# Order of the first transfers, of the key and query latents, and of the decays in a two-block transformer kernel

## The chip, the cores and the metric

The kernel runs on one core of a Trainium2 chip. The metric is the time of one execution on the device, in microseconds, as the median of several runs. Time before: 1764.14 us, median of 3 runs (1761.76 to 1773.75). Lower is better.

## The reference, cut to what matters

A first block of two layers (latent attention beside a gated mLSTM, then a convolutional feed-forward) works on 256 tokens of width 1024. A second block of one layer (linear attention, an RWKV recurrence and neighbourhood attention over a context of 256 tokens, then a mixture of 32 experts) follows. All numbers are float32. What the change touches is this:

```
silu_c, silu_cc = silu(c), silu(c_ctx)                 # one row of 1024 each
mod = silu @ ada_w + ada_b                             # 6 parts of 1024: shift, scale, gate, twice
h   = rms_norm(x) * gain * (1 + scale) + shift
# a mixer of the first block (two layers)
proj = h @ w_in                                        # c_q 384, c_kv 256, k_rope 32, q_m, k_m, v_m, o_m, i_m, f_m, gates
q  = (rms_norm(c_q)  @ w_uq ).reshape(.., 8 heads, 64 + 32);  q_rope  = rope(q[.., 64:])
kv = (rms_norm(c_kv) @ w_ukv).reshape(.., 8 heads, 64 + 64);  k_rope  = rope(k_rope)
y_mla   = softmax(q k^T / sqrt(96), masked by chunks of 64) @ v
y_mlstm = chunkwise mLSTM(silu(conv(q_m, k_m)), v_m, i_m, log_sigmoid(f_m))
          # cumulated log decays per head, running maxima, exp(decay) * (q k^T) @ v
x = x + gate * ((sigmoid(g) * (y_mla @ w1) + sigmoid(g') * (y_mlstm @ w2)) @ w_out)
```

The second block's context, `ctx_2`, goes through `mod`, `h` and a projection of its own; since it depends on nothing of the first block, the kernel does that first of all.

## The kernel before, in words

**Float32 by three products.** TensorE multiplies each operand as a rounded part and a rest: every weight tile of 128 rows and 1024 columns is split into `hi` (a cast on ScalarE, line 449) and `lo` (a difference on VectorE, line 451), and so are the activations. A product of a 128 by 128 weight block with 256 tokens is three matmuls (lines 472 to 474). Weights come from one long array in tiles of 2048 columns (1024 KB), through three buffers named `raw`; `Stream.take` loads a tile when it is first asked for and splits a half of it when that is first asked for.

**Modulation in the background.** `mod` is computed on VectorE: each 1024 KB tile of the `ada` matrix is loaded and multiplied with the activated row in two products with accumulation (line 532), each with a small read-out. Apart from the first two parts, this runs as a generator, one tile at a step; `tick()` moves it on by 0.8 tiles (first mixer) or 0.95 (second), and calls of `tick()` are spread over the mixer's text: one behind the norm, six in the latent stage, one per head, two per pair of heads in the mLSTM, four in the merge, four in the output projection. The tiles go through the same three `raw` buffers as the weights.

**Order.** The text of the program is not the order of the engines. When the program is built, a planner runs through it with modelled times and gives each engine, whenever that is free, the earliest instruction of the text that the model has as ready; each engine then works strictly in the order found. Loads of tiles stay in the order of the text on SyncE's queue. A table load that `pin()` asks for keeps its place in the text among the instructions of ScalarE.

**Start.** `context` (line 1157) activates the row `c_c` (`silu_row`, line 513: a transfer that spreads the row over all partitions, 512 KB, a tanh, a product, a halving), then runs eight modulation tiles through four buffers of their own. `vecs` (341.5 KB) and `ctxT` (1024 KB) are issued from ScalarE's queue, everything else from SyncE's. The second row, `c_x`, is activated behind the fourth tile (`CX_AT`). Then the context is normed (lines 589 to 593) and the joint projection of four columns begins, `proj4` (line 504), which takes the weights row by row so that it can start with the first normed block.

**Mixer** (line 659). *Latent stage:* `proj4` gives the three query latents and a fourth column that holds the gate inputs and k's rotary part (`p0`, `p1`); each latent is squared and scaled on ScalarE (`latent`, lines 683 and 684); `normed` (line 686) sums the squares by a matmul with ones, takes the root with logarithm and exponential, multiplies, and splits the result. Then the two key latents are projected (`p2`), evicted and normed. Four projections give q, two give k, one gives v. k's rotary part is spread to eight heads in one copy (line 728). *Decays* (lines 775 to 822): 26 VectorE instructions on 8 rows, some on other engines; they end in `rows`, `mcol` and `guard`, which only the mLSTM's pairs use. *Heads* (from line 839): scores, maximum, exponential, a step of the convolution generator (48 matmuls of projection, then convolution on VectorE), transposes and values. *Pairs* (line 873): the mLSTM. *Merge* (line 942) and *output projection* (line 960).

**PSUM.** The eight banks are shared out by tags: `d` two, `a` three, `y` two, `f` one. A bank holds two blocks of 256 tokens. `proj` and `proj4` use `d`.

The functions that the change touches:

## Time and profile before

| what | value |
|---|---|
| median of 3 runs | 1764.14 us |
| profiled execution, its own time | 1763.36 us |
| its span, first to last instruction | 1761.5 us |
| mean granted TensorE clock | 0.948 of full |
| busy: TensorE, VectorE, ScalarE, GpSimd | 1573.7, 1128.5, 756.8, 79.5 us |
| moved by DMA | 460.78 MB, mean 262 GB/s |
| the expert stage, 1310 to 1761 us | 403 GB/s, 0.99 of the DMA engines busy |

PE is TensorE, PEld its weight loads, DVE VectorE, ACT ScalarE, POOL GpSimd, SP SyncE. A busy TensorE is not one at its peak, since pipelined matmuls overlap in the record: the count of matmuls in a stretch tells more than the busy time. The clock is given as a share of full speed, 2.4 GHz; 0.5 is 1.2 GHz, and a mean between them is a stretch that had both. L472 is line 472 of the kernel before. In the rows below `<-` inside a name reads "written from", and in brackets behind an instruction stand the idle time before it and what ended it.

### The profile page before, as it was taken

How to read it: one execution, taken by the hardware profiler on the slowest of the kernel's cores; microseconds unless marked ns; L12 is line 12 of the kernel's file. 1: busy time of each engine (PE TensorE's matmuls, PEld its weight loads, DVE VectorE, ACT ScalarE, POOL GpSimd, SP SyncE). 2: the span in 40 equal slices, each digit the busy share in tenths (PEclk: the TensorE clock that was granted, in tenths of full speed). 3: DMA queues.
4: the chain of work that ended last, by engine and by line, in shares of the span. 5: the costliest groups of instructions: out<-in, count | busy, mean ns of one | idle time of the engine just before them, and what ended most of it. 6: DMA issues, size and time to landing. Idle time of an engine off the chain costs nothing.

```text
span 1761.5 us, 32047 instructions
## 1 busy us (share of the span) xinstructions
PE 1573.7 (89%) x13278; PEld 1267.9 (72%) x13278; DVE 1128.5 (64%) x2172; ACT 756.8 (43%) x1254; POOL 79.5 (5%) x81
## 2 busy tenths in 40 slices
PE   2988999999998899999999999999989867776766
PEld 2988999899998799989999999877874312221211
DVE  7998867798887998689988788757652111111011
ACT  3666545664455655556454566455531100000000
POOL 0000000020110000001011101000000000000000
PEclk7999999999999999999999999999989889887888
DMA  9846754556564678565667543223469999999998
GB/s 391 321 177 247 263 216 168 199 194 228 214 254 166 231 257 301 195 212 192 237 227 281 198 158 129 73 99 134 164 236 419 419 416 416 417 416 419 418 416 343
DMA packets 76807, 460.78 MB, mean 262 GB/s; under 512 B 8562, under 2 KB 11122, under 8 KB 28146
## 3 DMA queue, kind: packets, MB, share of 16 engines
q1 hardware_dynamic: 74064, 451.05, 67.1%
q10 hardware_dynamic: 2594, 7.64, 1.2%
q8 instruction: 106, 1.74, 0.4%
q14 instruction: 43, 0.35, 0.1%
HBM read 457.61 MB, written 1.05 MB: 260 GB/s over the span
## 4 chain that ended last, share of the span: by engine, by line
PE 65%; DMA 22%; DVE 8%; ACT 3%; issue 2%; SPq 0%; POOL 0%; DVEq 0%; ACTq 0%; POOLq 0%
DMA ew<-in_wgu 12%; PE d L472 11%; PE d L474 10%; PE d L473 10%; DMA ew<-in_wdown 7%; PE y L472 3%; PE y L474 3%; PE y L473 3%; PE a L1386 3%; DVE lo L451 2%; DVE raw L532 2%; PE d L2046 2%; PE a L1975 1%; PE d L485 1%; PE d L487 1%
## 5 line engine op out<-in xcount | busy, mean ns | idle before, releaser
L449 ACT CAST hi<-raw 128x1024 fp32r<-128x1024 f32 x309 | 322.5, 1049 | 307.5 <-PE d L473 178.8
L451 DVE TENSOR_TENSOR lo<-raw,hi 128x1024 fp32r<-128x1024 f32 x309 | 379.1, 1234 | 90.4 <-ACT hi L449 88.3
L472 PE MATMUL d<-hhi,hi 128*128 128x256 f32 x1352 | 396.9, 295 | 23.1 <-ACT hhi L590 20.8
L474 PE MATMUL d<-hhi,lo 128*128 128x256 f32 x1352 | 390.4, 289 | 5.3 <-DVE lo L451 5.3
L473 PE MATMUL d<-hlo,hi 128*128 128x256 f32 x1352 | 389.9, 289 | 2.2 <-DVE hlo L593 2.2
L472 PEld LDWEIGHTS d<-hhi,hi 128*128 128x128 f32 x1352 | 264.7, 196 | 31.7 <-ACT hhi L590 22.9
L474 PEld LDWEIGHTS d<-hhi,lo 128*128 128x128 f32 x1352 | 264.9, 196 | 7.8 <-DVE lo L451 6.5
L473 PEld LDWEIGHTS d<-hlo,hi 128*128 128x128 f32 x1352 | 265.2, 196 | 5.1 <-DVE hlo L593 2.9
L2046 PE MATMUL d<-ew,xe 128*32 128x512 f32 x984 | 167.9, 715 | 54.6 <-DMA ew<-in_wgu 54.2
L532 DVE SCALAR_TENSOR_TENSOR raw<-raw,cb 128x1024 f32<-128x1024 f32 x160 | 193.7, 1230 | 4.3 <-DMA raw<-in_ada 3.7
L2046 PEld LDWEIGHTS d<-ew,xe 128*32 128x32 f32 x984 | 26.4, 116 | 170.2 <-DMA ew<-in_wgu 145.6
L2051 DVE SCALAR_TENSOR_TENSOR moa<-moa,d 128x512 f32<-128x512 f32 x8 | 5.5, 688 | 179.8 <-ACT moa L2050 179.8
L2064 PE MATMUL y<-ew,mht 128*32 128x512 f32 x472 | 69.6, 652 | 28.8 <-DMA ew<-in_wdown 24.4
L2082 DVE SCALAR_TENSOR_TENSOR x<-f,mod_l,x 128x256 f32<-128x256 f32 x32 | 14.0, 479 | 126.3 <-PE f L2078 126.3
L457 POOL TENSOR_TENSOR hidl<-fgel,hidh 128x256 fp32r<-128x256 f32 x44 | 56.0, 1272 | 830.1 <-ACT hidh L456 765.1
L472 PE MATMUL y<-hhi,hi 128*128 128x256 f32 x320 | 91.6, 286 | 0.8 <-ACT hi L449 0.8
L474 PE MATMUL y<-hhi,lo 128*128 128x256 f32 x320 | 90.9, 285 | 0.8 <-DVE lo L451 0.8
L473 PE MATMUL y<-hlo,hi 128*128 128x256 f32 x320 | 90.6, 283 | 0.0
L2050 ACT ACTIVATE moa<-d 128x512 f32<-128x512 f32 x8 | 4.8, 597 | 186.1 <-PE d L2046 186.1
L2064 PEld LDWEIGHTS y<-ew,mht 128*32 128x32 f32 x472 | 12.8, 115 | 76.5 <-DMA ew<-in_wdown 56.0
L472 PEld LDWEIGHTS y<-hhi,hi 128*128 128x128 f32 x320 | 61.3, 192 | 1.4 <-ACT hi L449 1.0
L474 PEld LDWEIGHTS y<-hhi,lo 128*128 128x128 f32 x320 | 61.2, 192 | 1.4 <-DVE lo L451 1.0
(676 smaller groups left out, 3187.4 us busy)
## 6 DMA issues: line engine op xcount, KB each, us to landing
raw<-in_ws SPq DMA_DIRECT2D x151, 1024.0 KB, 4.9
ew<-in_wgu SPq DMA_DIRECT2D x100, 1024.0 KB, 18.0
raw<-in_ada SPq DMA_DIRECT2D x80, 1024.0 KB, 4.9
ew<-in_wdown SPq DMA_DIRECT2D x46, 1024.0 KB, 19.7
ew<-in_wgu SPq DMA_DIRECT2D x46, 512.0 KB, 13.8
ew<-in_wdown SPq DMA_DIRECT2D x28, 512.0 KB, 12.6
two<-in_wgu SPq DMA_DIRECT2D x20, 256.0 KB, 8.4
two<-in_wdown SPq DMA_DIRECT2D x16, 256.0 KB, 7.9
```

The lines of the kernel that those rows point to most:

```text
L449: f.append(nc.scalar.copy(hi_, raw))
L451: f.append(nc.vector.tensor_tensor(lo_, raw, hi_.bitcast(F32), OP.subtract))
L457: (eng or self.nc.vector).tensor_tensor(lo, src, hi.bitcast(F32), OP.subtract)
L472: nc.tensor.matmul(out, whi, hhi, start=first and i == 0, stop=False, **s)
L473: nc.tensor.matmul(out, whi, hlo, start=False, stop=False, **s)
L474: nc.tensor.matmul(out, wlo, hhi, start=False, stop=last and i == n - 1, **s)
L485: nc.tensor.matmul(out, hhi[:, tok], whi, start=first and i == 0 and not (t and shared), stop=False, **s)
L487: nc.tensor.matmul(out, hlo[:, tok], whi, start=False, stop=last and i == n - 1, **s)
L532: nc.vector.scalar_tensor_tensor(w, w, 1.0, c, OP.mult, OP.mult, accum_out=mod[:, j : j + 1])
L1386: nc.tensor.matmul(ps[r, g * 64 : g * 64 + 64], l_(g, p, r), r_(g, p, r), start=True, stop=True, skip_group_check=True)
L2046: nc.tensor.matmul(ps[32 * e : 32 * e + 32, :], xe[:, k, 32 * e : 32 * e + 32], w[e], start=k == 0, stop=k == 7, skip_group_check=True)
L2064: nc.tensor.matmul(py[q][32 * e : 32 * e + 32, :], ht[:, f * P + 32 * e : f * P + 32 * e + 32], w[e], start=f == 0, stop=f == 3, skip_grou ...
```

## The change

At the start, `vecs` and `ctxT` are issued on SyncE's queue behind the second modulation tile; the first weight tile of the context projection is loaded and its first half split behind the sixth tile (`Stream.reach`); the row `c_x` is loaded and activated behind the eighth. The halving in `silu_row` is gone, and the products of `ada` halve instead.

In each mixer the columns of the latents are reordered: `proj4` gives the two key latents and two query latents; the third query latent and the gate column follow in a bank of tag `y`. Key latents are normed there and then; the first half of k is projected, then the query latents are normed, then come the second half of k, its rotary part, v, and last q. The weights of `uq` are packed in that order. The six calls of `tick()` of the latent stage are gone. The decays are a function that is called in the second head (`hd == 1`), between the convolution step and the values; only their first four instructions stay in the latent stage.

```
--- before.py
+++ after.py
@@ _lat_cols
-    return r(0) + r(7) + z(24) + r(8) + z(24) + kr + kr[16:] + kr[:16] + r(1)
+    return r(1) + r(0) + r(7) + z(24) + r(8) + z(24) + kr + kr[16:] + kr[:16]
@@ prep
-        w.add("uq" + s, _tblk(f["w_uq"][l], _uq_cols()), _tblk(ukv[:, :512]), _tblk(ukv[:, 512:], n=512))
+        w.add("uq" + s, _tblk(ukv[:, :512]), _tblk(ukv[:, 512:], n=512), _tblk(f["w_uq"][l], _uq_cols()))
@@ class Stream
     def take(self, w=P):
 
-        net, a = self.net, self.pos
+        o = self.reach(self.pos)
         self.pos += w
+        assert o + w <= 1024
+        return self.hi[:, o : o + w], self.lo[:, o : o + w]
+
+    def reach(self, a=0):
+        net = self.net
         c, o = a // 2048, a % 2048
...
             self.hi, self.lo = net.split_w(self.raw[:, 1024 * b : min(1024 * b + 1024, self.width)])
-        o %= 1024
-        assert o + w <= 1024
-        return self.hi[:, o : o + w], self.lo[:, o : o + w]
+        return o % 1024
@@ silu_row
         nc.vector.scalar_tensor_tensor(t, th, 1.0, t, OP.add, OP.mult)
-        nc.vector.tensor_scalar(t, t, 0.5, None, OP.mult)
@@ ada
-                    nc.vector.scalar_tensor_tensor(w, w, 1.0, c, OP.mult, OP.mult, accum_out=mod[:, j : j + 1])
+                    nc.vector.scalar_tensor_tensor(w, w, 0.5, c, OP.mult, OP.mult, accum_out=mod[:, j : j + 1])
@@ mixer
-        raw = mt([8, T], "raw", F32, "kf")
+        raw = mt([8, T], "raw", F32, "qf")
...
-        def normed(dst, j, n, d):
+        def normed(dst, j, n, d, pin=True):
...
-            self.rstd(r, o, d)
+            self.rstd(r, o, d, pin=pin)
...
-        p0, p1 = self.proj4(st, h)
-        latent(0, p0[:, :T], self.V("qn" + s, 0))
-        latent(1, p0[:, T:], self.V("qn" + s, 1))
-        latent(2, p1[:, :T], self.V("qn" + s, 2))
-        self.tick()
-
+        pkv, p01 = self.proj4(st, h)
+        for q in range(2):
+            latent(3 + q, pkv[:, q * T : q * T + T], self.V("kvn" + s, q))
+        for q in range(2):
+            latent(q, p01[:, q * T : q * T + T], self.V("qn" + s, q))
+        p2 = self.ps("y")
+        self.mm3(p2[:, :T], st, h)
+        normed(ckv, 3, 2, 256)
+        latent(2, p2[:, :T], self.V("qn" + s, 2))
+        self.mm3(p2[:, T:], st, h)
+
+        cqp, ckvp = self.parts(cq, range(3)), self.parts(ckv, range(2))
+        kf, vn = mt([8, T], "kf"), mt([2, 512], "vn")
+        st = Stream(self, "uq" + s)
+
+        def keys(b):
+            pq = v2(self.proj(st, ckvp))
+            nc.scalar.copy(kf[0:64, 4 * b : 4 * b + 4 : 2, :], pq[0:64])
+            nc.vector.tensor_copy(kf[0:64, 4 * b + 1 : 4 * b + 4 : 2, :], pq[64:128])
+
+        keys(0)
+        normed(cq, 0, 3, 384, False)
+
+        krm = mt([T], "krm")
+        nc.vector.tensor_tensor(krm[64:128, :], p2[64:128, T:], self.cs[64:128, :], OP.mult)
         gi, gf = self.tmp(T, "gi", bufs=1, rows=8), self.tmp(T, "gf", bufs=1, rows=8)
-        nc.vector.tensor_scalar(gi, p1[0:8, T:], self.V("gb" + s)[0:8], None, OP.add)
-        nc.vector.tensor_scalar(gf, p1[32:40, T:], self.V("gb" + s)[32:40], None, OP.add)
-        krm = mt([T], "krm")
-        nc.vector.tensor_tensor(krm[64:128, :], p1[64:128, T:], self.cs[64:128, :], OP.mult)
-        self.tick()
-        normed(cq, 0, 3, 384)
-        p2 = self.proj(st, h)
-        for j in range(2):
-            latent(3 + j, p2[:, j * T : j * T + T], self.V("kvn" + s, j))
-        self.tick()
-        normed(ckv, 3, 2, 256)
+        nc.vector.tensor_scalar(gi, p2[0:8, T:], self.V("gb" + s)[0:8], None, OP.add)
+        nc.vector.tensor_scalar(gf, p2[32:40, T:], self.V("gb" + s)[32:40], None, OP.add)
+        keys(1)
         pk = self.ps("a")
         nc.tensor.matmul(pk[:, :T], self.C("rep")[64:128, :], krm[64:128, :], start=True, stop=True)
+        nc.scalar.copy(kf[64:128], bcn(pk[64:128, :T], 8))
+        pv = [self.ps("d") for _ in range(2)]
+        self.mm3n(pv, st, ckvp, 512, False)
+        for i in range(2):
+            nc.scalar.copy(vn[:, i, :], pv[i])
+        qf = mt([8, T], "qf")
+
+        lf, e1 = gf, self.tmp(T, "e1", bufs=1, rows=8)
+        nc.vector.tensor_scalar(e1, gf, -1.0, None, OP.mult)
+        nc.vector.tensor_tensor(e1, e1, gf, OP.min)
+        nc.scalar.activation(e1, e1, AF.Exp)
+        nc.scalar.activation(e1, e1, AF.Ln, bias=self.one[:8])
         for b in range(4):
             pq = v2(self.proj(st, cqp))
             nc.scalar.copy(qf[0:64, 2 * b : 2 * b + 2, :], pq[0:64])
             nc.vector.tensor_tensor(qf[64:128, 2 * b : 2 * b + 2, :], pq[64:128], bcn(self.cs[64:128, :], 2), OP.mult)
-            if b == 1:
-                nc.scalar.copy(kf[64:128], bcn(pk[64:128, :T], 8))
-            if b % 2:
-                self.tick()
-        for b in range(2):
-            pq = v2(self.proj(st, ckvp))
...
-        pv = [self.ps("d") for _ in range(2)]
-        self.mm3n(pv, st, ckvp, 512, False)
...
-        self.tick()
...
-        lf, e1 = gf, self.tmp(T, "e1", bufs=1, rows=8)
...
-        nc.vector.tensor_scalar(lf, gf, 0.0, None, OP.min)
...
-        nc.scalar.activation(guard, mcol[:, 1], AF.Exp)
+        rows, mcol, guard = mt([384], "mrows", F32R), mt([2, 2, 8], "mcol"), mt([2, 8], "guard")
+
+        def decays():
+            nc.vector.tensor_scalar(lf, gf, 0.0, None, OP.min)
...
+            nc.scalar.activation(guard, mcol[:, 1], AF.Exp)
...
             next(conv, None)
+            if hd == 1:
+                decays()
             self.pv(py, e, vn, hd)
             self.tick()
@@ context
             cc = self.silu_row(A["c_c"], nc.sync)
-            nc.scalar.dma_start(self.vec, A["vecs"])
             xc = cx.tile([P, 8, T], F32, name="xc")
-            nc.scalar.dma_start(xc, A["ctxT"].rearrange("p (k t) -> p k t", k=8))
+            st = Stream(self, "cx")
             for i, _ in enumerate(self.ada(A["ada2"], cc, self.V("adab2", 0, 48), self.mod_c, (0, 1), cx)):
-                if i == CX_AT:
-                    self.cb = self.silu_row(A["c_x"], nc.sync)
-            if CX_AT > 7:
-                self.cb = self.silu_row(A["c_x"], nc.sync)
+                if i == 1:
+                    nc.sync.dma_start(self.vec, A["vecs"])
+                    nc.sync.dma_start(xc, A["ctxT"].rearrange("p (k t) -> p k t", k=8))
+                if i == 5:
+                    st.reach()
+            self.cb = self.silu_row(A["c_x"], nc.sync)
             h = self.norm_mod(xc, self.V("n1", 0, 8), self.mod_c[:, 8:16], self.mod_c[:, 0:8], False)
-            st = Stream(self, "cx")
```

## Rows read from the trace of the kernel before

**Rows 1.** Windows: start:end, length, then busy us (instructions) of PE, PEld, DVE, ACT, POOL; clock; DMA.
```profile
0.00:10.00 10.00, 0.00 (x0) 0.00 (x0) 2.77 (x14) 2.34 (x2) 0.19 (x4) 1.00 0.81 290
...
20.00:30.00 10.00, 0.00 (x0) 0.00 (x0) 8.85 (x16) 2.25 (x2) 0.00 (x0) 0.56 1.02 424
...
122.00:156.00 34.00, 27.21 (x166) 24.37 (x164) 29.12 (x50) 23.54 (x37) 0.00 (x0) 0.85 0.65 247
156.00:200.00 44.00, 41.37 (x326) 39.01 (x325) 41.55 (x88) 26.39 (x56) 0.00 (x0) 1.00 0.62 223
284.00:313.00 29.00, 28.40 (x238) 27.97 (x238) 24.71 (x37) 15.24 (x19) 0.00 (x0) 1.00 0.51 182
579.00:605.00 26.00, 22.24 (x159) 20.55 (x157) 25.31 (x43) 19.31 (x32) 0.00 (x0) 0.93 0.69 254
605.00:620.00 15.00, 11.18 (x59) 9.76 (x59) 12.25 (x28) 6.85 (x14) 0.00 (x0) 0.77 0.59 221
737.00:767.00 30.00, 29.40 (x246) 28.98 (x246) 25.41 (x44) 15.79 (x21) 0.00 (x0) 1.00 0.51 176
```

**Rows 2.** Chain of waits, first 41 us: start, us, engine, tile, line, pieces.
```profile
3.43 16.41 DMA cb<-in_c_x
...
22.29 1.23 DVE cb L519
...
25.27 8.03 DVE raw L532 x14
...
33.81 2.07 DVE two L589 x5
...
39.44 1.15 DVE lo L451
40.63 0.58 PE d L474
```

**Rows 3.** Timeline of TensorE, first mixer: start, us, instruction, idle before and releaser.
```profile
122.38 0.28 PE L473 MATMUL d<-hlo,hi 128*128 128x256 f32 x1
122.50 0.28 PE L474 MATMUL d<-hhi,lo 128*128 128x256 f32 x1
...
126.95 0.58 PE L472 MATMUL d<-hhi,hi 128*128 128x256 f32 x1 [0.57 <-ACT hi L449]
...
149.59 0.39 PE L472 MATMUL d<-lat,hi 128*128 128x256 f32 x1 [1.87 <-DVE qf L726]
```

**Rows 4.** Timeline of ScalarE, latent stage of the first mixer.
```profile
122.15 0.38 ACT L683 ACTIVATE sqk<-d 128x256 f32<-128x256 f32 x1 [6.98 <-PE d L474]
...
124.19 1.28 ACT L540 ACT_TABLE_LOAD   x1
...
129.12 0.83 ACT L456 CAST lat<-raw 128x768 fp32r<-128x768 f32 x1
...
145.16 1.87 ACT L728 COPY kf<-a 64x2048 f32<-64x2048 f32 x1
```

**Rows 5.** Timelines of ScalarE and TensorE in the expert stage, around 1365 us.
```profile
1365.01 0.37 ACT L1991 COPY selT<-a 128x256 f32<-128x256 f32 x1 [12.05 <-PE a L627]
...
1365.43 0.61 PE L1993 MATMUL a<-ones,selw 128*128 128x1 f32 x4 [0.46 <-ACT selT L1991]
```

**Rows 6.** Windows of line 532 alone (modulation products and read-outs): VectorE, clock, DMA.
```profile
122.00:156.00 34.00, 7.26 (x12) 0.85 0.65 247
...
284.00:313.00 29.00, 0.00 (x0) 1.00 0.51 182
579.00:605.00 26.00, 8.18 (x14) 0.93 0.69 254
```

**Rows 7.** Timelines of VectorE and TensorE, second mixer, decays and first head.
```profile
600.63 0.41 DVE L776 TENSOR_TENSOR gf<-gf,e 8x256 f32<-8x256 f32 x1
...
611.04 1.13 DVE L813 TENSOR_TENSOR mrows<-mrr,mrows 8x384 fp32r<-8x384 f32 x2
...
612.97 0.47 PE L627 MATMUL a<-kon,esm 128*128 128x128 f32 x1 [3.82 <-ACT esm L851]
```

More of the change, by code (lines that the diff above doesn't have):

```diff
@@ L31 @@
 OUT_RATES = (0.4, 1.0, 1.0, 0.5)
-CX_AT = 3
 HG, MID_FIRST, MID_BUFS, RK_SECOND = "fy", 3, 4, (3, 0)
@@ L722, in mixer @@
-        st = Stream(self, "uq" + s)
+        nc.scalar.copy(kf[64:128], bcn(pk[64:128, :T], 8))
[8 more added lines that the diff above has]
+        nc.scalar.activation(e1, e1, AF.Exp)
@@ L726, in mixer @@
             nc.vector.tensor_tensor(qf[64:128, 2 * b : 2 * b + 2, :], pq[64:128], bcn(self.cs[64:128, :], 2), OP.mult)
-            if b == 1:
-                nc.scalar.copy(kf[64:128], bcn(pk[64:128, :T], 8))
-            if b % 2:
-                self.tick()
-        for b in range(2):
-            pq = v2(self.proj(st, ckvp))
-            nc.scalar.copy(kf[0:64, 4 * b : 4 * b + 4 : 2, :], pq[0:64])
-            nc.vector.tensor_copy(kf[0:64, 4 * b + 1 : 4 * b + 4 : 2, :], pq[64:128])
-        pv = [self.ps("d") for _ in range(2)]
-        self.mm3n(pv, st, ckvp, 512, False)
-        for i in range(2):
-            nc.scalar.copy(vn[:, i, :], pv[i])
-        self.tick()
         qk, vm = mt([8, T], "qk"), mt([2, 8, 65], "vm")
@@ L767, in conv @@
                 yield
-        lf, e1 = gf, self.tmp(T, "e1", bufs=1, rows=8)
-        nc.vector.tensor_scalar(e1, gf, -1.0, None, OP.mult)
-        nc.vector.tensor_tensor(e1, e1, gf, OP.min)
-        nc.scalar.activation(e1, e1, AF.Exp)
-        nc.scalar.activation(e1, e1, AF.Ln, bias=self.one[:8])
-        nc.vector.tensor_scalar(lf, gf, 0.0, None, OP.min)
-        nc.vector.tensor_tensor(lf, lf, e1, OP.subtract)
-        b = self.tmp(T, "bcum", bufs=1, rows=8)
-        nc.vector.tensor_tensor_scan(b, self.C("reset")[:8], lf, 0.0, OP.mult, OP.add)
@@ L788, in mixer @@
-        nc.vector.tensor_copy(sml[:, 4:8], cml)
-        bl = self.tmp(4, "mbl", bufs=1, rows=8)
-        nc.vector.tensor_copy(bl, blast)
-        nc.vector.tensor_tensor_scan(sml[:, 1:4], sml[:, 4:7], bl[:, 0:3], 0.0, OP.max, OP.add)
-        nm = gi
-        nc.vector.tensor_tensor(ch(nm), ch(cm), sml[:, 0:4].unsqueeze(2).to_broadcast([8, 4, 64]), OP.max)
-        nc.vector.scalar_tensor_tensor(ng, nm, -1.0, b, OP.mult, OP.subtract)
-        nc.vector.tensor_scalar(nm, nm, -1.0, None, OP.mult)
@@ L796, in mixer @@
-        off = self.tmp(16, "moff", bufs=1, rows=8)
-        ov = off.rearrange("p (c d) -> p c d", c=4)
-        nc.vector.memset(off, NEG)
-        for c in range(4):
-            nc.vector.memset(ov[:, c, c : c + 1], 0.0)
-            if c:
-                nc.vector.tensor_scalar(ov[:, c, :c], ov[:, c - 1, :c], bl[:, c - 1 : c], None, OP.add)
-        rows, rr = mt([384], "mrows", F32R), self.tmp(384, "mrr", bufs=1, rows=40)
-        nc.gpsimd.memset(rows.bitcast(F32), 0.0)
-        c4 = lambda t: t.rearrange("p (c s) -> p c s", s=64)
@@ L807, in mixer @@
-        for g in range(2):
-            r = slice(32 * g, 32 * g + 8)
-            for i, at in enumerate((0, 4)):
-                nc.vector.tensor_tensor(c4(rr)[r, at : at + 4 - 2 * i], ch(nm)[:, 2 * i :],
-                                        ov[:, 2 * i :, 2 * i + g].unsqueeze(2).to_broadcast([8, 4 - 2 * i, 64]), OP.add)
-            nc.scalar.copy(rows[r, :], rr[r, :])
-            nc.vector.tensor_tensor(rows[64 + 32 * g : 72 + 32 * g, :], rr[r, :], rows[r, :].bitcast(F32), OP.subtract)
@@ L814, in mixer @@
-        nc.gpsimd.memset(vm[:, :, :, 64:], 1.0)
-        pm = self.ps("a")
-        for k in range(2):
-            for i in range(2):
-                self.transpose(pm[:, (2 * k + i) * 8 : (2 * k + i) * 8 + 8], mrow[:, k * T + i * P : k * T + i * P + P])
-        mcol = mt([2, 2, 8], "mcol")
-        nc.vector.tensor_copy(mcol, pm[:, :32].rearrange("p (k i h) -> p k i h", k=2, i=2))
-        guard = mt([2, 8], "guard")
-        nc.scalar.activation(guard, mcol[:, 1], AF.Exp)
+        rows, mcol, guard = mt([384], "mrows", F32R), mt([2, 2, 8], "mcol"), mt([2, 8], "guard")
```

54 lines of the change are left out of this document (43 added, 11 removed).

## The prediction

> **What bounds the kernel now.** I read the busy times by stage first, then the chain of waits for the first 41 us, then TensorE's own timeline where a stage holds fewer matmuls than its length would take. The reader is to compare counts, not busy time. At full clock one 256-column matmul follows the other at 0.12 us [rows 3]. The latent stage of the first mixer holds 166 matmuls in 34.00 us [rows 1]; at that pace they take 19.9 us, so 14.1 us are lost there. The same stage of the second mixer holds 159 in 26.00 us (19.1 us at that pace, 6.9 lost), and the 15.00 us behind it, with the first head, hold 59 at a mean clock of 0.77 (7.1 us at that pace, 7.9 lost) [rows 1]. The last figure flatters the loss by some 1.4 us, since 12 of these matmuls are 512 wide: 6.5. So about 27 us of the two mixers are TensorE waiting or running at 1.2 GHz. In the first mixer its stream stops at 122.50 and is taken up at 126.95, because latents are evicted, squared and normed before anything else can be multiplied; later it waits 1.87 us for a VectorE copy of q [rows 3]. In the second it waits 3.82 us for the softmax of the first head, with the last of the decays just ahead on VectorE [rows 7]. VectorE is the second bound: 41.55 busy of 44.00 us in the first heads, 24.71 of 29.00 and 25.41 of 30.00 in the two merge stages [rows 1].
>
> The start is a chain of its own: the transfer of c_x, its activation, modulation products back to back, the norm, a low part of the first weight tile, and only at 40.63 the sustained stream of matmuls [rows 2].
>
> **The change, part by part.**
>
> *Start.* Ahead of the last modulation products now stand c_c (0.52 MB), vecs (0.35), ctx (1.05), eight tiles of 1.05 and, new, the first weight tile of 1.05; c_x goes behind them. That is 11.4 MB. The core moved 2.9 MB in its first 10 us and 424 GB/s later, with SyncE's queue alone at work from 20 to 30 us [rows 1], so putting vecs and ctx on that queue costs no bandwidth. By these rates the eighth tile lands at about 30. A product with its read-out takes 1.15 us (7 of each are the 14 pieces of 8.03 us), so its two end 2.3 us later; bias and gain took 0.5 (33.30 to 33.81), and the norm's first product starts at about 32.8 against 33.81 [rows 2]: 1.0 us. VectorE no longer sets this time, so the halving pass that is dropped there (over the same 1024 columns as the product of 1.23 us [rows 2], so at most that, twice here and once in the feed-forward) is worth nothing by itself. The larger part is the weight tile: it is split during the modulation products, so the stream need not wait for the low part (1.15 us, up to 40.6 [rows 2]). TensorE can then run its stream once the first low part of the normed context exists, five products and one more step of 0.41 us behind the start (2.5 us), at 35.3, against 40.63 less the 0.8 us of four matmuls done before: 4.5 us. Against it stands c_x: a table load, its tanh and its product of 1.23 us [rows 2] now fall among the norm's first instructions, and on SyncE its transfer stands behind a tile that waits for a buffer. I take **-4 us**, with ends of -1 (only the norm's advance) and -7. vecs and ctx land later by some 2 us; the bias and a sum of squares need them, some 10 us later.
>
> *Latent stage.* Key latents come first, and 48 matmuls (5.8 us) of the third query column and the gate column follow into a bank that needs no eviction. ScalarE evicts four latents instead of three (three took 122.15 to 124.19, 2.04 us [rows 4], so 2.7), loads a table (1.28 [rows 4]), and only then the third query latent (0.7): 4.7 us behind the joint projection.
>
> The gate column is written into the other half of the PSUM bank from which ScalarE reads that query latent. What this does shows elsewhere in the trace: a one-column matmul into a bank began 0.05 us after ScalarE's copy out of other columns of it, having waited 0.46 us [rows 5]. So I let the gate column wait: 24 matmuls take 2.9 us, the eviction ends at 4.7, a stop of about 2 us.
>
> The Trainium skill has the rule (PSUM — Partial Sum Buffer, "PSUM bank collisions raise a hardware error"): guard PSUM by bank and quadrant, not by address, so disjoint columns of a bank are no protection. By that rule the stop stands; if it did not hold, the 48 matmuls would run through and the sum below would be -17 instead of -13. The trace agrees with it, by the 0.46 us above.
>
> The norm of key latents runs meanwhile. Before, the cast of the normed latents began 7.0 us behind the first eviction [rows 4]; with the cast and its difference, 0.8 each, that is 8.6, and the gate column ends at 4.7 + 2.9 = 7.6. So the keys may wait 1 us more. Then the values wait for both key evictions, which may stand behind the 1.87 us copy of k's rotary part [rows 4], 1.0; the queries wait for the values' eviction, 0.6 (an estimate: a quarter of that copy's columns, and some start), and for their own, 0.9. 5.5 us of loss remain. First mixer: 14.1 - 5.5, **-8.5 us**, ends -3 and -12. Second: 6.9 + 6.5 - 5.5, less 2 for a stop that the decays make at head two instead of head one, **-6 us**, ends -2 and -10.
>
> *Decays.* 26 VectorE instructions, from the one at 600.63 to the pair at 611.04 [rows 7], 6.8 us in all, now come in one block inside the second head, where VectorE has 2.45 us free in 44.00 [rows 1]. Behind them on VectorE wait the next head's maximum and the convolution; the cover is that head's 48 matmuls. Part of them (in the second mixer the pair at 611.04) ran among the heads before. First mixer **+1.5 us** (0 to 5); the second's is in the figure above.
>
> *Six ticks less per mixer.* Each tick moves the modulation stream on by 0.8 or 0.95 of a tile. It took 7.26 and 8.18 us of VectorE in the latent stages [rows 6], which become free. The stream is not shorter: it ends six ticks later, and about three tiles (6 products, 7 us) reach into the merge stage, which had none [rows 6] and where VectorE has 4.3 and 4.6 us free [rows 1]. Overflow 3 us, part of it taken up by the output projection behind: **+2 us** per mixer, +4 (0 to 8); if that cover were gone, the whole 7 would be on the path. The same holds for transfers: three raw buffers serve weights and modulation tiles alike, so the latent stage's weights lose a rival and the merge's gain one; nothing.
>
> Sum: -4 - 8.5 - 6 + 1.5 + 4 = **-13 us** on the profiled execution's 1763.36 (its span of 1761.5 and 1.9 around it), which is 0.8 us under the median of the runs. All of it lies ahead of the expert stage, whose transfers start from where the work before them ends, so it passes to the end. I say 1750.
>
> **The rivals.**
>
> A, *the moved work fits*: merge and heads take it into VectorE's idle time (for it: the lagging stream leaves the heads less modulation work too), so +5.5 falls away and the start gains up to 7: 1742 to 1745. Without the wait within the bank it would be 4 less, 1738. Chance 0.20.
>
> B, *handed back, or not done as written*: the order on an engine is laid out by a planner's modelled times. It may put the queries' norm ahead of the keys', or ScalarE's evictions and casts pace the stage. Then the latent stages give 3 and 2, the start 3, and the costs stay: -8 + 5.5, about 1761. Against it: the gate column needs nothing but one eviction. Chance 0.20.
>
> C, *VectorE becomes the bound in heads and merge*, slower: the decays' 6.8 and the stream's 7 lie on the path whole in both mixers (28 us), and each pause sends the clock to 1.2 GHz as the first head of the second mixer had it (0.77 over 15 us, some 3.4 us [rows 1]), twice. With B's gains of 8: 28 + 7 - 8 = +27, about 1790. It decides once the block needs more than the free time of the first heads. For it: 2.45 us free of 44.00 [rows 1]. Against: part of the decays ran there before. Chance 0.07, most of it beyond 1%.
>
> **How the numbers follow.** The forecast has 0.53, and a range of its own of 1741 to 1760. A change within 1%, 17.6 us, can't be told from none by a measurement of this kernel; the limits are 1746.5 and 1781.8. Faster: nearly all of A and a third of the forecast, 0.38. Slower: 0.05. Same: 0.57. The range of 1734 to 1765 takes in A, the forecast and most of B.
>
> **What would show it.** In the changed kernel's trace: the sustained matmuls start near 35 to 36 us, with the first weight's low part ahead of the norm's products; after each mixer's joint projection 24 matmuls, a stop of about 2 us that an eviction ends, 24 more, then keys; no 3.82 us stop before the first softmax, but a shorter one behind the second head; no modulation products in the latent stages and about six in each merge; the clock at 2.4 GHz through both latent stages. It is wrong if the stop before the keys is as long as the old one (4.45 us), or if TensorE's waits for VectorE in the merge exceed 4 us.

## The result, and where the time went

The changed kernel takes 1773.01 us (median of 12 runs, 1764.24 to 1778.01) against 1761.89 (12 runs) for the kernel before: a ratio of 1.0052, 95% interval 1.0031 to 1.0074 (ratios here weigh all runs of both kernels; the medians alone would give 1.0063). It is slower by half a per cent, 23 us above the forecast of 1750 and 8 above the top of the range of 1734 to 1765. Its profiled execution took 1772.79 us with a span of 1770.9, 9.4 more than before. One run of 3644.1 us, of the kernel with the decays ahead of the heads, is left out of that kernel's ratio.

To find 9.4 us, cut both traces at the same events and subtract. The marks here are the context's last matmul, the first matmul of each mixer, its first head, its first pair, its merge, the last update of x, the next norm, the first expert matmul and the end. All lengths are in us.

| stretch | before | after | difference | forecast |
|---|---|---|---|---|
| start, to the context's last matmul | 108.4 | 110.2 | +1.8 | -4, with the next row |
| from there to the first mixer's first matmul | 0.8 | 5.7 | +4.9 | |
| first mixer, to the first head | 46.8 | 37.2 | -9.6 | -8.5 |
| its heads; its pairs | 69.0; 59.0 | 70.0; 58.7 | +1.0; -0.3 | +1.5; 0 |
| its merge and output projection | 48.4 | 51.4 | +3.0 | +2 |
| feed-forward | 231.6 | 231.2 | -0.4 | 0 |
| second mixer: norm to first head; heads | 40.8; 75.4 | 38.6; 69.8 | -2.2; -5.6 | -6 in all |
| its pairs | 57.5 | 57.6 | +0.1 | 0 |
| its merge and output projection | 48.8 | 59.5 | +10.7 | +2 |
| feed-forward | 235.0 | 235.5 | +0.5 | 0 |
| second block, up to the experts | 296.4 | 301.3 | +4.9 | 0 |
| experts | 443.8 | 444.2 | +0.4 | 0 |

The latent stages won what was forecast, or a little more. Three places lost more than forecast: the start (+6.7 instead of -4), the second mixer's merge and projection (+10.7 instead of +2) and the second block, whose text is untouched (+4.9 instead of 0).

The windows of the changed kernel (columns as in [rows 1]) show two of the three:

```profile
116.00:153.00 37.00, 33.28 (x240) 31.12 (x241) 28.52 (x50) 25.88 (x43) 0.00 (x0) 0.96 0.33 117
153.00:223.00 70.00, 67.32 (x545) 64.20 (x545) 63.01 (x128) 40.26 (x84) 0.00 (x0) 1.00 0.67 245
282.00:309.00 27.00, 24.79 (x204) 24.01 (x203) 26.86 (x43) 13.38 (x17) 0.00 (x0) 1.00 0.68 245
730.00:759.00 29.00, 26.79 (x207) 25.95 (x207) 25.60 (x41) 13.21 (x18) 0.00 (x0) 0.94 0.68 249
759.00:790.00 31.00, 27.55 (x198) 26.45 (x196) 22.67 (x41) 13.99 (x16) 0.00 (x0) 0.89 0.60 209
1180.00:1223.00 43.00, 40.54 (x379) 32.20 (x377) 31.04 (x56) 24.63 (x44) 2.12 (x2) 0.84 0.37 135
```

The first two rows are the first mixer up to its first head, and its heads. In the kernel before the same two stretches were:

```profile
109.00:156.00 47.00, 38.74 (x255) 35.51 (x255) 40.70 (x77) 28.92 (x48) 0.00 (x0) 0.89 0.61 230
156.00:225.00 69.00, 66.35 (x530) 63.03 (x529) 61.70 (x125) 39.23 (x82) 0.00 (x0) 1.00 0.68 245
```

The stretch up to the first head holds 240 matmuls in 37 us at a clock of 0.96, where it had 255 in 47 at 0.89. So 15 matmuls (1.8 us at 0.12 each) did not become cheaper but moved behind the first head: the heads hold 545 instead of 530. In the first merge VectorE is busy for 26.86 of 27 us, and in the second merge and projection the clock falls to 0.94 and 0.89. The last row of the first group is a stage of the second block. Its counterpart in the kernel before, which no earlier group shows, has about as many matmuls at full clock:

```profile
1177.00:1215.00 38.00, 35.42 (x383) 28.12 (x383) 30.93 (x57) 25.01 (x45) 2.41 (x3) 1.00 0.44 159
```

*The start.* TensorE's timeline of the changed kernel (start, duration, tiles; in brackets the idle time before and what ended it; two pieces):

```profile
35.82 0.80 PE L474 MATMUL d<-hhi,hi 128*128 128x256 f32 x2 [14.79 <-ACT hhi L591]
38.00 0.58 PE L475 MATMUL d<-hlo,hi 128*128 128x256 f32 x1 [1.38 <-DVE hlo L594]
...
51.95 0.28 PE L476 MATMUL d<-hhi,lo 128*128 128x256 f32 x1
54.08 0.39 PE L474 MATMUL d<-hhi,hi 128*128 128x256 f32 x1 [1.85 <-ACT cpad L1216]
...
109.73 0.81 PE L572 MATMUL f<-two,ones 128*128 128x256 f32 x3
115.87 0.79 PE L474 MATMUL d<-hhi,hi 128*128 128x256 f32 x2 [5.33 <-ACT hhi L591]
```

The stream does start earlier, at 38.00 against 40.63 [rows 2], and at 46 us TensorE has begun 62 matmuls against 48. Then it stops for 1.85 us until ScalarE has evicted the first bank, and once more for 5.33 us ahead of the first mixer. ScalarE's timeline of the changed kernel names both causes:

```profile
48.99 2.20 ACT L561 ACTIVATE two<-x 128x512 f32<-128x512 f32 x4 [1.51 <-DMA x<-in_xT]
51.10 1.03 ACT L451 CAST hi<-raw 128x1024 fp32r<-128x1024 f32 x1
52.15 1.28 ACT L541 ACT_TABLE_LOAD   x1
53.44 1.08 ACT L1216 COPY cpad<-d 128x512 f32<-128x512 f32 x2
...
111.26 1.28 ACT L548 ACT_TABLE_LOAD   x1
112.56 0.47 ACT L548 ACTIVATE rstd<-f,eps 128x256 f32<-128x256 f32 x1
113.05 1.28 ACT L549 ACT_TABLE_LOAD   x1
114.34 0.42 ACT L549 ACTIVATE rstd<-rstd 128x256 f32<-128x256 f32 x1
```

The evictions (`cpad`) stand in ScalarE's list behind three things: four squares of x, which wait for x's transfer, then a weight cast, then a table load of 1.28 us. And the root for x's norm is taken only at 112.56; before it was at 81.6. The sum behind it, by the tile's rows of the changed kernel and then of the kernel before (durations, first and last start):

```profile
L572 PE MATMUL f<-two,ones x8: 377/378/379, 79.0 to 110.2; 128*128 128x256 f32 x8
```

```profile
L571 PE MATMUL f<-two,ones x8: 377/378/379, 59.8 to 78.9; 128*128 128x256 f32 x8
```

This reduction belongs to the first mixer's text. The planner had put it into holes of the context; the changed list has its last pair behind the context's last matmul, so root, products and casts follow with TensorE empty.

*The merge.* Modulation products in the changed kernel's three stretches 282 to 309, 730 to 759 and 759 to 790, which held 0, 0 and 1 before:

```profile
L533 DVE SCALAR_TENSOR_TENSOR raw<-raw,cb x6: 1218/1219/1220, 283.0 to 302.7; 128x1024 f32<-128x1024 f32 x6
...
L533 DVE SCALAR_TENSOR_TENSOR raw<-raw,cb x6: 1218/1219/1223, 731.6 to 753.8; 128x1024 f32<-128x1024 f32 x6
...
L533 DVE SCALAR_TENSOR_TENSOR raw<-raw,cb x3: 1218/1218/1220, 762.4 to 788.4; 128x1024 f32<-128x1024 f32 x3
```

What SyncE's queue waited for in the second merge, 725 to 765 us (total, times, longest):

```profile
SPq L442 <- DVE lo L453: 26.3, 6, 7.9
SPq L442 <- DVE raw L533: 13.7, 3, 8.1
```

and, in the first merge (276 to 300 us), the queue's wait for modulation products, the transfers themselves, and ScalarE:

```profile
SPq L442 <- DVE raw L533: 11.8, 2, 8.1
...
276.68 5.15 SPq L442 DMA_DIRECT2D raw<-in_ada  x2
290.03 1.47 SPq L442 DMA_DIRECT2D raw<-in_ws  x2
```

```profile
294.11 0.63 ACT L458 CAST hhi<-mga 128x512 fp32r<-128x512 f32 x1 [5.89 <-DVE mga L959]
294.90 1.99 ACT L451 CAST hi<-raw 128x1024 fp32r<-128x1024 f32 x2 [0.16 <-DMA raw<-in_ws]
```

Two of the three `raw` buffers held modulation tiles. The next weight tile could be issued only at 290.03, when VectorE let one go after 8.1 us, landed for the cast at 294.90, and TensorE stood for 1.2 us (at 296) behind that cast. The chain goes VectorE, buffer, transfer, ScalarE, TensorE; TensorE's own row names only its last link.

### The profile page after: what moved, and what is told of

It reads as the page before. It is cut to its first block, busy times and chain, and to the rows that moved or that the text cites. A ratio compares the mean times of both kernels' runs of the same rounds, so it can differ in the third digit from the quotient of the medians.

```text
span 1770.9 us, 32054 instructions
## 1 busy us (share of the span) xinstructions
PE 1579.1 (89%) x13278; PEld 1269.7 (72%) x13278; DVE 1128.0 (64%) x2167; ACT 758.6 (43%) x1256; POOL 77.9 (4%) x81
## 4 chain that ended last, share of the span: by engine, by line
PE 63%; DMA 23%; DVE 8%; ACT 4%; issue 2%; POOL 0%; SPq 0%; DVEq 0%; ACTq 0%; POOLq 0%
DMA ew<-in_wgu 11%; PE d L474 10%; PE d L476 10%; PE d L475 10%; DMA ew<-in_wdown 8%; PE y L474 4%; PE y L476 3%; PE y L475 3%; PE a L1392 3%; DVE lo L453 2%; PE d L2052 2%; DVE raw L533 2%; PE a L1981 1%; PE a L628 1%; DMA raw<-in_ws 1%
## 5 line engine op out<-in xcount | busy, mean ns | idle before, releaser
L474 PE MATMUL d<-hhi,hi 128*128 128x256 f32 x1320 | 387.9, 295 | 29.4 <-ACT hhi L591 23.7
L475 PE MATMUL d<-hlo,hi 128*128 128x256 f32 x1320 | 381.3, 289 | 3.2 <-DVE hlo L594 1.7
L476 PE MATMUL d<-hhi,lo 128*128 128x256 f32 x1320 | 380.2, 288 | 0.2 <-DVE lo L453 0.2
L474 PEld LDWEIGHTS d<-hhi,hi 128*128 128x128 f32 x1320 | 258.4, 196 | 38.3 <-ACT hhi L591 26.3
L475 PEld LDWEIGHTS d<-hlo,hi 128*128 128x128 f32 x1320 | 259.3, 196 | 6.6 <-DVE hlo L594 2.9
L2052 PE MATMUL d<-ew,xe 128*32 128x512 f32 x984 | 165.3, 704 | 56.5 <-DMA ew<-in_wgu 56.0
L474 PE MATMUL y<-hhi,hi 128*128 128x256 f32 x352 | 100.8, 286 | 4.6 <-ACT raw L685 3.9
L476 PE MATMUL y<-hhi,lo 128*128 128x256 f32 x352 | 100.0, 285 | 0.9 <-DVE lo L453 0.9
L475 PE MATMUL y<-hlo,hi 128*128 128x256 f32 x352 | 99.6, 283 | 0.0
L474 PEld LDWEIGHTS y<-hhi,hi 128*128 128x128 f32 x352 | 67.4, 192 | 6.1 <-ACT raw L685 4.7
L476 PEld LDWEIGHTS y<-hhi,lo 128*128 128x128 f32 x352 | 67.4, 192 | 1.4 <-DVE lo L453 1.1
```

The source lines that it names most:

```text
L474: nc.tensor.matmul(out, whi, hhi, start=first and i == 0, stop=False, **s)
L475: nc.tensor.matmul(out, whi, hlo, start=False, stop=False, **s)
L476: nc.tensor.matmul(out, wlo, hhi, start=False, stop=last and i == n - 1, **s)
L2052: nc.tensor.matmul(ps[32 * e : 32 * e + 32, :], xe[:, k, 32 * e : 32 * e + 32], w[e], start=k == 0, stop=k == 7, skip_group_check=True)
```

## The experiments

All are edits of the changed kernel (the start alone: of the kernel before). Ratios are to the kernel before, with the 95% interval. The kernel before, run beside them, had medians of 1762.0 to 1762.4. The stage columns come from each profile, which is one execution, in us: when the first head begins, first merge and projection, second mixer from its norm to its merge, second merge and projection, second block.

| run | median | ratio | first head at | merge 1 | mixer 2 | merge 2 | block 2 | span |
|---|---|---|---|---|---|---|---|---|
| before | 1761.89 | | 156.0 | 48.4 | 173.7 | 48.8 | 296.4 | 1761.5 |
| changed | 1773.01 | 1.0052 (1.0031 to 1.0074) | 153.1 | 51.4 | 166.0 | 59.5 | 301.3 | 1770.9 |
| start only | 1765.54 | 1.0024 (1.0000 to 1.0047) | 158.6 | 48.3 | 174.2 | 48.8 | 294.8 | 1762.7 |
| mixers only | 1767.64 | 1.0020 (0.9995 to 1.0045) | 147.1 | 52.5 | 166.0 | 59.3 | 294.9 | 1761.5 |
| x's sums early | 1767.49 | 1.0017 (0.9993 to 1.0041) | 148.8 | 56.6 | 166.0 | 57.1 | 304.8 | 1772.2 |
| sums behind evictions | 1766.24 | 1.0012 (0.9992 to 1.0033) | 146.3 | 53.5 | 166.0 | 56.5 | 305.5 | 1767.4 |
| ticks back | 1774.56 | 1.0067 (1.0041 to 1.0093) | 154.4 | 48.4 | 178.1 | 48.8 | 295.1 | 1772.4 |
| stream in pairs | 1760.50 | 0.9986 (0.9961 to 1.0011) | 144.6 | 48.4 | 173.0 | 47.3 | 295.1 | 1749.8 |
| decays before heads | 1775.39 | 1.0051 (1.0023 to 1.0079) | 156.0 | 52.3 | 166.1 | 56.5 | 305.1 | 1772.0 |
| a bank each | 1771.75, one run | | 152.8 | 52.8 | 163.3 | 58.3 | 305.1 | 1770.0 |
| pairs and banks | 1747.58 | 0.9910 (0.9884 to 0.9937) | 145.1 | 48.3 | 172.1 | 47.3 | 295.0 | 1747.3 |
| the same, start mended | 1750.86 | 0.9923 (0.9893 to 0.9952) | 146.1 | 48.6 | 170.7 | 47.3 | 294.9 | 1746.9 |
| the same, three ticks | 1753.97 | 0.9939 (0.9916 to 0.9962) | 145.8 | 48.3 | 165.9 | 49.3 | 306.6 | 1753.7 |
| the same, changed start | 1757.68 | 0.9979 (0.9955 to 1.0004) | 153.6 | 48.6 | 170.6 | 47.3 | 294.8 | 1753.8 |

Medians are of 12 runs, except ticks back and decays before heads (10), three ticks (9), pairs and banks and the same with the mended start (6 each). A median mixes the stages with the second block, which in the profiles takes 294.8 to 296.4 us in eight kernels and 301.3 to 306.6 in six; so the stage columns decide between theories, and medians only where they agree with them.

**Start only.** All start edits of the diff, made in the kernel before.

> The kernel before with the start of the changed kernel alone (order of the first transfers, early first weight tile, c_x last, no halving); mixers as before. In the changed kernel's profile the first mixer's first matmul comes 6.7 us later than before (115.87 against 109.15), after a TensorE stop of 5.5 us: the reduction of x for the first norm was laid behind the last matmul of the context, where it had stood among them before. Theory: the start alone costs 6 to 9 us; forecast 1769 us (1766 to 1773) against 1761.9 before, with the stop of about 5 us at 110 us in its profile. Rival: the start is innocent and the mixers are what costs, through the modulation products that now stand in the merge: then 1757 to 1762.

The profile has the stop; this is TensorE's row of it:

```profile
115.72 0.80 PE L475 MATMUL d<-hhi,hi 128*128 128x256 f32 x2 [5.33 <-ACT hhi L592]
```

It came out at 1765.54, half the expected cost and between the two theories. The first mixer's first matmul comes 6.6 us later, the first head only 2.6: beside the later start the old latent stage is 4.0 us shorter (42.8 against 46.8), since TensorE's stops in it come to 4.5 us instead of 8.1. So the start costs, but less beside the old mixers than beside the new; on the total alone, an interval of 1.0000 to 1.0047, it could be nothing.

**Mixers only.** The same edits undone in the changed kernel.

> The changed kernel with the start of before put back (first transfers, c_x behind the fourth tile, halving); its mixers stay changed. Theory: from the first norm to the end of the output projection the first mixer gains about 7 us and loses 3 in the merge, the second gains 7 and loses 4 to 10 in merge and projection, so about -4 in all; forecast 1758 us (1753 to 1763), and up to 1764 if the granted clock falls to 0.5 behind 1190 us again, as it did for 13.7 us in the changed kernel's profile. Rival: the mixers are what costs; then 1770 or more here.

By stages the theory holds in kind: the first head is 8.9 us early, the second mixer 7.7 shorter, and most of both is handed back by the merges (+4.1 and +10.5 with the projections). But the forecast missed: the span equals that of before, to 0.1 us, and the median, 1767.64, lies above the forecast's 1753 to 1764 and even above its own profile's 1763.34, which no stage explains. It does not reach the rival's 1770.

**x's sums early.**

```
+            self.r0 = self.rstd_x(self.x)          # behind the context's first projections
...
-        return self.scaled(x, self.rstd_x(x, adds), gain, shift)
+        return self.scaled(x, r or self.rstd_x(x, adds), gain, shift)
```

> The changed kernel, with the sum of squares of x and its root written right behind the context's first three projections instead of at the head of the first mixer; nothing else. Theory: the start costs because that reduction is the last thing on TensorE's list before the mixer, so this gives back the 5.5 us stop and the matmuls at half clock behind it: 1767 us (1764 to 1769) against 1773. Rival: the start costs because VectorE's list there is fuller (c_x's product inside the norm, two products of modulation ahead of a low part at 52 us, a stop of 2 us); the place of the reduction only shows it; then 1771 to 1774.

1767.49: the theory's value. The first head comes 4.3 us earlier than in the changed kernel, and the 5.33 us stop is gone. The profile's span, 1772.2, does not show that gain (its execution took 1774.03 us, the longest of the 12): the first merge and projection take 5.2 us more, with 6.8 us at 1.2 GHz from 307.5, and the second block 3.5 more. The stop for the bank is longer, because the squares still stand ahead of the eviction:

```profile
54.27 0.39 PE L474 MATMUL d<-hhi,hi 128*128 128x256 f32 x1 [2.79 <-ACT cpad L1217]
```

**Sums behind evictions.** The same, and:

```
-            self.r0 = self.rstd_x(self.x)
+            with self.tc.issue_after(evicted):     # the second eviction to cpad
+                self.r0 = self.rstd_x(self.x)
```

> The run with the early sum of squares of x, with that sum tied behind ScalarE's eviction of the context's first two banks. In the changed kernel these evictions stood behind four squares of x that waited 1.5 us for x's transfer, and TensorE stopped 1.9 us at 52 us until they came, then ran 3.4 us at half clock; with the early sum it stopped 2.8 us there. Theory: with evictions first the stop goes, and the lead of 14 matmuls that the early weight tile gave at 46 us is kept: 3 to 4 us less than with the early sum alone, 1764 us (1760 to 1766) against 1767.5. Rival: the context is bound by its weights' transfers and splits, so the lead is lost by 60 us anyway: 1766 to 1769.

The stop at 52 us is gone, the first head is another 2.5 us earlier, and the lead reached 19 matmuls at 75 us (303 begun against 284 before). But the lead was then lost: at 85 us it was 344 against 360. TensorE's row:

```profile
78.38 0.39 PE L474 MATMUL d<-hhi,hi 128*128 128x256 f32 x1 [1.43 <-DMA raw<-in_ada]
```

So theory and rival are each half right, and the time, 1766.24, is on the rival's edge. With both stops mended, the first head is 0.8 us earlier than with the start of before (146.3 against 147.1). That is all the new order of transfers is worth.

**Ticks back.**

```
+        self.tick()                                 # six places in the latent stage, as before
```

> The changed kernel with the six ticks of the latent stage put back, so that about five modulation tiles are worked off there again. Theory: merge (26.7 and 28.2 us long against 24.0 before) and second output projection (31.3 against 24.8) get back what they lost, since the six products in each of them go away, and the latent stages lose less than that: 1767 us (1762 to 1771). Rival: VectorE's time in the latent stage is worth as much as in the merge: each product of 1.23 us put back there delays a norm or an eviction, and the time stays at 1771 to 1776 with merges of 24 us.

The rival was right. Merges and projections return to 48.4 and 48.8 us, the 14 us that they lost, but the first mixer's heads take 74.8 us instead of 70.0, and the second mixer up to its merge takes 12.1 more. VectorE's time is as dear in latent stage and heads as in the merge.

**Stream in pairs.** Mixers only, and in the pairs:

```
                 next(gates)
             self.tick()
+            for _ in range(2 if l and pair == 0 else 1):
+                self.tick()
```

> Changed mixers with the start of before (as in the run of the mixers alone), and four more ticks in the mLSTM's pairs of the first mixer, five in the second, so that the modulation stream ends there. In the run of the mixers alone the second mixer's merge began 11.7 us earlier than before, and at the end of its output projection 1.3 us were left; VectorE was busy 39.8 of 59 us in the first pairs, 44.9 of 58 in the second, and 26.0 of 27 and 25.1 of 28 in the merges. Theory: the lead is handed back because the stream's last tiles stand in merge and projection; with them in the pairs, merges of 24 us, a projection of 25, and 1752 us (1747 to 1757). Rival: the tiles share three buffers and the DMA with the weights, so the pairs (TensorE 58.8 busy of 59 us) get longer by what the merges save: 1762 to 1768.

The windows of its first pairs, first merge and first projection:

```profile
213.00:272.00 59.00, 58.86 (x489) 56.77 (x488) 46.85 (x75) 29.86 (x46) 0.00 (x0) 1.00 0.78 294
272.00:296.00 24.00, 23.62 (x200) 23.39 (x199) 20.13 (x30) 13.67 (x18) 0.00 (x0) 1.00 0.51 176
296.00:321.00 25.00, 24.77 (x205) 24.51 (x205) 18.26 (x32) 13.22 (x16) 0.00 (x0) 1.00 0.58 204
```

In the first mixer the theory holds exactly: the pairs stay at 59 us with VectorE at 46.85 instead of 39.8, and the merge takes 24.0. In the second the rival has a part: its pairs grow by 6 us (63.6 against 57.6) while merge and projection win 12.0. The profiled execution took 1751.54 us; the median of 1760.50 is above the forecast's range, since four of the 12 runs lie at 1767 to 1769.

**Decays before heads.**

```
+        decays()                                    # ahead of the first head
...
-            if hd == 1:
-                decays()
```

> The changed kernel with the block of decays called ahead of the first head instead of in the second. Theory: the place in the second head is worth something: the first softmax waits for the block again, by 3 to 4 us in each mixer as it did in the second mixer before (3.82 us), so 1777 us (1774 to 1781) against 1773, and the stop inside the second head goes away. Rival: the stop only moves (the block takes 6.8 us of VectorE wherever it stands in the heads): 1771 to 1774.

By stages the rival was right that the place is worth nothing: the first head begins 2.9 us later, the heads take 67.1 us instead of 70.0, and the first pair begins at 223.1 us in both. The median, 1775.39, lies in the theory's range, but its interval and the changed kernel's overlap. Neither foresaw why: no stop for the decays shows on TensorE in either place (the longest in the first mixer's heads is 0.8 us with the block there, 0.9 with it ahead). The later first head is 22 matmuls that the planner now laid ahead of it (262 against 240).

**A bank each.**

```
-        p2 = self.ps("y")
-        self.mm3(p2[:, :T], st, h)
+        p2, p3 = self.ps("y"), self.ps("y")
+        self.mm3(p3[:, :T], st, h)                  # third query latent; the gate column stays in p2
```

> The changed kernel with the third query latent and the gate column in a bank each instead of the two halves of one. Theory: the stop ahead of the gate column (2.2 us in each mixer, ended by ScalarE's eviction out of the other half) is a wait for the bank, and goes; the keys then wait up to 1 us for their normed latents, so the heads begin 1 to 1.5 us earlier after each mixer's norm, 2 to 3 us in all. Rival: the stop is one for the weights' low part (on VectorE until 134.5 us) or for the order laid out, and stays.

TensorE's rows at the gate column, in the changed kernel (first and second mixer) and with banks apart:

```profile
134.47 0.38 PE L474 MATMUL y<-hhi,hi 128*128 128x256 f32 x1 [1.92 <-ACT raw L685]
...
584.43 0.38 PE L474 MATMUL y<-hhi,hi 128*128 128x256 f32 x1 [1.98 <-ACT raw L685]
```

```profile
131.68 0.59 PE L692 MATMUL f<-sqk,ones 128*128 128x256 f32 x2
131.92 0.47 PE L474 MATMUL y<-hhi,hi 128*128 128x256 f32 x1
```

The stop was the bank's, and it goes. What it frees shows elsewhere than I expected: the first heads are not earlier, but the heads take 67.0 us instead of 70.0 and 69.8. The planner filled the freed time with matmuls of the heads: the first mixer's heads hold 529 instead of 545. From a mixer's first matmul to its first pair the gain is 1.8 us in the first mixer, and from the norm 2.7 in the second. One run decides nothing on the total.

**Pairs and banks**, the last two edits together.

> Start of before, changed mixers, the modulation stream ended in the pairs, and the third query latent and the gate column in a bank each: the two edits of the mixers together. With the banks apart the profile of the changed kernel showed latent stages of unchanged length (21.1 us from the first sum of squares to the first head) but heads of 67 us instead of 70 in both mixers. Theory: both edits take different losses and add up, 3 us a mixer below the stream's run (1760.5): 1755 us (1750 to 1759). Rival: the 3 us of the heads are work moved out of them that stands elsewhere, since the first mixer's merge was 1.4 us longer in that profile: 1759 to 1762.

1747.58, faster than the kernel before by 0.9% (0.6 to 1.2), and below the range that was expected. The heads take 67.1 and 67.0 us, and merge and projection 48.3 and 47.3. By profiles it is 2.5 us below the stream's run; the rest of the 13 us between the medians is not explained by any stage.

**The same with the mended start.**

> The run of pairs and banks, with the changed start and the sum of squares of x early and behind the evictions. That start led by 19 matmuls (2.3 us) at 75 us and had lost them at 85 us, behind a stop of 1.4 us and 3.4 us at half clock. Theory: the context is bound by its weights' transfers and splits from 75 us on, so the start is worth nothing once its two stops are gone: within 2 us of the run of pairs and banks. Rival: the stop at 76 us was that run's own bad luck with the clock, and the 2.3 us last: 2 to 4 us less than that run.

1750.86. The profile is 0.4 us shorter (span 1746.9 against 1747.3) and the intervals overlap; the medians differ by 3.3 us, more than the theory's 2, and in the direction away from the rival. So no gain of the mended start shows.

**The same with three ticks instead of five** in the second mixer's pairs.

> The run of pairs and banks with three more ticks instead of five in the second mixer's pairs. In that run the second mixer took 66.4 us from its first pair to the merge, against 57.6 with the changed mixers alone, and merge and projection 47.3 against 59.2. Theory: five are too many, since DMA and VectorE (56 of 67 us) then pace the pairs; with three the pairs fall by 3 to 5 us and at most one tile reaches the merge: 2 to 4 us less, 1744 us (1741 to 1748). Rival: what is saved in the pairs is lost in merge and projection, where each product costs TensorE as much: 1746 to 1750.

Pairs, merge and projection of the second mixer take 109.9 us together instead of 113.7, as the theory had it. But the second block took 306.6 us instead of 295.0 in the profile, and the median is 1753.97. So the total went against me, for a reason outside the edit.

**The same with the changed start, not mended.**

> The changed kernel, start included and untouched, with the stream ended in the pairs (four and five more ticks) and the banks apart. Theory: the changed start costs its 5.3 us stop at 110 us and the half clock behind it, whatever the mixers do: 5 to 7 us above the run of pairs and banks (1747.6), 1754 us (1750 to 1757). Rival: the start cost nothing in itself, and the half clock of 13.7 us in the middle of the changed kernel was what its runs showed: within 2 us of 1747.6.

The stop of 5.33 us is there, at 110.7 to 116.0 us, and the first head is 8.5 us later. The profile is 6.5 us longer (span 1753.8 against 1747.3), within the theory; the median is 10 longer, and the intervals of the ratios don't meet. So beside these mixers too the start costs its stop.

## Why the prediction was wrong, step by step

**Start, "I take -4 us": this step failed.** The stream began at 38.00 and not 35.3, 2.6 us earlier than before where 4.5 were worked out. The norm's first product began at 34.74 and not 32.8: VectorE waited 1.19 us for a cast of the weight tile and made both its low parts (2.36 us) ahead of the last four modulation products. But the sign came from something I did not look at. I followed VectorE and SyncE and never asked what stands on ScalarE's list behind x's transfer (a stop of 1.85 us), nor what happens to work that the planner had laid into holes (a stop of 5.33 us): both stood at nothing in the sum. In the kernel before, x's sum stood among the context's matmuls at 60 to 79 us, by a row I had not read. Runs that move that sum alone (1767.49), mend both stops (1766.24), and keep the start beside better mixers (1757.68 against 1747.58) show it: with the new mixers the first head comes 6.0 and 8.5 us later as changed, and 0.8 earlier to 1.0 later when mended.

**Latent stages, -8.5 and -6: right.** -9.6, of which 1.8 is the 15 matmuls that moved behind the first head, and -7.8 with the heads. The order came as written, the clock was at full but for 3.4 us at the start of each, and the stop by the bank was 1.92 and 1.98 us against "about 2". The other terms of the 5.5 us of loss came out otherwise: the keys did not wait, and the values waited 1.67 us instead of 1.0. The rule of the Trainium skill (PSUM — Partial Sum Buffer, "PSUM bank collisions raise a hardware error"), to guard PSUM by bank and quadrant and not by address, stood behind that stop. The trace agrees: 1.92 and 1.98 us with both halves in one bank, none with a bank each. That the hardware would raise an error is not shown by any run here.

**Decays, +1.5: near in number, by luck.** The heads grew by 1.0 us, but with 15 matmuls more in them (1.8 us). TensorE's idle time in the first mixer's heads is as before (2.68 us against 2.65), and the shorter stop that was to come behind the second head is in neither mixer. So the decays found room on VectorE (with the ticks back, the same heads took 74.8 us), and their place did not matter: ahead of the heads the first pair begins at the same time.

**Ticks, "+2 us per mixer": mechanism right, size wrong in the second mixer.** There are six products in each merge, as forecast, but in the second mixer two more than before in the projection. (I put that down to its higher rate of 0.95 tiles a tick; no run tests it.) The stretch lost 10.7 us instead of 2. The sentence that failed is the one on transfers: "the latent stage's weights lose a rival and the merge's gain one; nothing". Weight tiles came late through the shared buffers, TensorE paused, and its clock was at 1.2 GHz for 3.4 us from 747.3 and 6.8 us from 764.4; by these 10.2 us at half speed, the clock is some 5 of the 10.7 (an estimate). The first merge paused as long behind weight casts (1.7 us against 1.6), kept 2.4 GHz and lost 3.0; why the clock fell in one and not in the other is not shown. Emptied of products, the merges took 24.0 us again, with the ticks back and with the stream in the pairs (22.5 there in the second mixer).

My test for the merge, TensorE waiting for VectorE for over 4 us, would have passed it: the waits that name VectorE are 0.6 and 0.7 us there. The wait stands further back: TensorE waits for ScalarE's cast, the cast for a transfer, and the transfer was issued late, after 8.1 us of SyncE's waiting for a buffer that a modulation product held.

**"So it passes to the end": off by 4.9 us in the profile**, all in the second block and by the granted clock (last section). Whether the change causes that is open.

**Rivals.** A was right for the heads, which took the decays in, and wrong for merge and start. C named the right resource in the merge and the clock after it, but placed it in the heads too, where TensorE waited no longer than before. B said that the gains would be handed back: they were, but by the merges, not by the order in the latent stages. The result is within 1% of before, which had 0.57; the range missed by 8 us.

## What to carry to other kernels

Before moving transfers at a start, list what stands on each in-order engine behind every one of them, and what an automatic layout has filled into holes of that stretch: a reduction that was free in a hole cost 5.3 us at the end. Background work that is taken out of one stage comes back in another, so put it where the bottleneck engine has cover (here the pairs, with 13 to 19 us free on VectorE; even there the second mixer's grew by 6 us), before counting the gain of the stage that it left. And follow a wait back through its engines to the one that holds a shared buffer.

## What the runs showed of the hardware

TensorE's clock differed in a stage whose lists of instructions are the same in all these kernels. Each profile has a TensorE stop of 1.6 to 1.9 us there, before the same matmul, which starts between 1171 and 1200 us. Behind it the granted clock stayed at 2.4 GHz in the kernel before (3.4 us at 1.2 fell near the block's start there, at 1024.7), was at 1.2 for 3.4 us in seven others, and at 1.2 for 13.7 to 17.1 us in six, among them the changed kernel; the block took 294.8 to 296.4 us in the first eight and 301.3 to 306.6 in the six. The clock fell 0.5 to 0.8 us after the stop's end in the seven, and 0.9 to 2.0 us after it in the six, 2.0 in the changed kernel. That goes with the length in all 13 profiles; no experiment moved it by itself, so what decides it stays open.

It is not tied to the start: the run with three ticks has the start of before and the long stretch. Nor does the kernel alone seem to fix it: of the nine executions with three ticks one took 1743.46 us at a mean clock of 0.955, the others 1751.65 to 1755.49 at 0.942 to 0.945 (the clock by stage is on record for one execution only). It is why a gain of 4 us in one stage can be invisible in the median, and why the 4.9 us of the changed kernel's second block can't be put down to the change.
